# Hybrid encoder step on one core: two weights' splits moved ahead of the first evictions

## The chip, the core and the metric

The kernel is one launch on one core of a Trainium2 chip. The metric is the device time of that launch in microseconds (us). Most executions of one kernel agree within about 0.3%. The engines are TensorE (PE: matmuls; PEld: its weight loads), VectorE (DVE), ScalarE (ACT), GpSimd (POOL) and SyncE (SP). Each works through its own queue in order. SP and POOL issue the DMAs of this kernel's weights.

## What is computed

One step of an encoder layer, for a prompt of 512 rows and a sample of 64 rows, 576 rows side by side:

```python
x += mixer(rmsnorm(x))        # gated DeltaNet branch || GLA branch, gated merge
x += cross_attn(rmsnorm(x))   # 4 heads into 256 memory tokens
x += conv_ffn(rmsnorm(x))     # up-projection, causal conv, gate, down-projection
y  = rmsnorm(x)
```

This study deals with the first 45 us. There `h = rmsnorm(x)` (model width 1024) and `proj = h @ w_in` begin, whose columns are q, k, v, z and so on, by heads of 128. The first three products are q, k and v of head 0, the fourth is z of head 0, and the fifth and sixth are value heads of the GLA branch. A narrow product of 32 columns (gates and low-rank gate input) stands between the third and the fourth.

## The kernel before

**Tiles.** Activations lie transposed: 8 tiles of 128 features x 576 rows. Every operand of a projection is kept as a high and a low part (`h` rounded to fp32r, `lo` the rest), and a product is made of three: high x high, high x low of the activation, low x high of the weight. A weight of 128 columns is 8 blocks of 128x128, so one tile of 128x1024 for `h` and one for `lo`. The 576 columns go as 256 and 320 into two PSUM banks, so a projection is 8 blocks x 3 x 2 = 48 matmuls. The norm's factor per row is applied when a product is evicted, so products of the first norm don't wait for it.

**How a weight is made** (`emit_weight`, `split_summed`). SP loads it into a raw tile (`wr`, 4 buffers). ACT writes `-raw`, rounded, into `lo` (ACTIVATE in the trace) and then `raw`, rounded, into `h` (CAST). POOL then issues a DMA from HBM that adds the weight onto `lo` (`w<-wt` in the trace), so that what is left in `lo` is the weight less `h`. The weight tiles (`w`) have 6 buffers, so three weights at a time. A new weight's tile has to wait until TensorE has read what lay in that buffer. The first three weights are split by ACT and DVE alone, in six halves beside the loads of x.

```python
def split_summed(h, lo, raw, src):
    A.activation(lo, raw, AF.Copy, scale=-1.0)
    A.copy(h, raw)
    drv.accumulate(lo, src, nc.gpsimd)
```

**Order.** Instructions are not issued where they are written. A driver (`Driver`) keeps a model of when each operand is ready and each engine free, puts each instruction into a heap with its modelled start, and empties the heap in that order (line 292, to which the profile puts nearly everything). So the code's order fixes what the model may see, and the model fixes the order on each engine. `pending` holds the tiles that are still in use for the driver: `drop` gives tiles back, `fetch` emits the next weights as long as fewer than 6 weight tiles are in use, and `weight` drops the tiles of weights that went before and emits what is missing.

**The start** (`main`, from line 1760). `first3` are the PSUM tiles of the first three products. They run with the block k as the outer loop, and the weights are repacked so that the first weight tile holds what the first 48 of the 144 matmuls need, the second the next 48, the third the last 48. Behind them `conv_raw` evicts the three products (two by DVE, one by ACT, tiles `u`), `fetch(3)` asks for more weights, and `sq_act` squares the last four tiles of x (ACT) and adds them up into `acc` (DVE). `c_rstat` makes the norm's factors: matmuls of `acc` with ones, `rin` (DVE), the power `rt` (POOL), two diagonal tiles `dg` (DVE), matmuls of `dg` with ones, and `rbc` (ACT). `c_first` then makes `ba` (DVE) from the narrow product and `rbc`, and `c_gates` multiplies it on TensorE (`sm<-cst,ba` and `sm<-ba,wg`).

At `fetch(3)` all 6 weight tiles are still in use for the driver, so it emits nothing. The fourth, fifth and sixth weight are emitted when the fourth product (`za`) asks for its weight, which is after the evictions, the squares and the narrow product in the code.

Of the kernel before, what the change touches and what calls it, by code (L numbers as in the profile page):

```python
# [22 lines left out]
KT = D // P  # L23
# [489 lines left out]
def tile_trunk(ctx, tc, xT, memT, wt, wd, vec, cst, w0, wgate, st_gdn, st_conv, st_gla, st_ffn, ckT, cv,  # L513
# [23 lines left out]
    def slot(s="s", dt=F32, w=SLOT):  # L537
        return drv.rotate("s", NS, sp.tile([P, w], dt, tag="s", name=nm(s)))
# [36 lines left out]
    def f(ap):  # L575
        return ap.bitcast(F32)
# [3 lines left out]
    wready = {}  # L580
# [5 lines left out]
    def drop(*aps):  # L586
        for ap in aps:
            drv.pending.discard((ap if hasattr(ap, "tensor") else ap[:]).tensor.name)

    def raw_tile():  # L590
        while all(n in drv.pending for tag in ("raw", "rawf") for n in drv.ring.get(tag, ())) and len(drv.ring.get("raw", ())) == RAWB:
            make(next(iter(unmade)))
        if fp is not None and drv.first("rawf", RF, "raw", RAWB):
            return keep(drv.rotate("rawf", RF, fp.tile([P, 1024], F32, tag="rawf", name=nm("wr"), bufs=RF)))
        return keep(drv.rotate("raw", RAWB, wp.tile([P, 1024], F32, tag="raw", name=nm("wr"), bufs=RAWB)))
# [3 lines left out]
    def w_tile():  # L599
        if fp is not None and drv.first("wf", WF, "w", WB):  # L600
            t_ = drv.rotate("wf", WF, fp.tile([P, 1024], F32R, tag="wf", name=nm("w"), bufs=WF))
        else:
            t_ = drv.rotate("w", WB, wp.tile([P, 1024], F32R, tag="w", name=nm("w"), bufs=WB))
        wnames.add(t_[:].tensor.name)
        return keep(t_)
# [8 lines left out]
    def defer(i, fn, at):  # L614
        if i < LATE0:
            fn()
            return
        unmade[i] = fn
        drv.later(at, lambda: make(i))

    def emit_weight(i, at=0.0):
        kind, idx = WORDER[i]
        if kind == "*":
            wready[i] = emit_product(i, at, *idx)
            return
        raw = raw_tile()
        n = 1024
        if kind == "dn":
            m, p = idx
            n = len(PARTS[p]) * 128  # L630
            src = wd[m, :, PART0[p] * 128:PART0[p] * 128 + n]
        elif kind in ("outa", "outb"):
            n, c = 512, 512 * (kind == "outb")
            src = wt[WIDX[("out", idx)], :, c:c + 512]
        else:
            src = wt[WIDX[(kind, idx)]]
        DMA(raw[:, :n], src)
        h = w_tile()
        h, lo = (h[:, 0:512], h[:, 512:1024]) if n <= 512 else (h[:], w_tile()[:])
        summed = kind in SUMMED and (kind, idx) != ("dn", (7, 3))  # L640

        def split_():
            if summed:
                split_summed(h[:, :n], lo[:, :n], raw[:, :n], src)
            else:
                A.copy(h[:, :n], raw[:, :n])
                X.tensor_tensor(lo[:, :n], raw[:, :n], f(h[:, :n]), op=ALU.subtract)
            drop(raw[:])

        defer(i, split_, max(drv.ready_at(raw[:, :n]), at - (LEADD if summed else LEADV)))  # L650
        wready[i] = (h, lo)
# [5 lines that stand above are left out]
# [76 lines left out]
    def fetch(i, now=None):  # L733

        now = i if now is None else now
        room = WB + (WF if fp is not None else 0)
        for j in range(i, len(WORDER)):
            if j in wready:
                continue
            if j >= wlimit[0]:  # L740
                break
            kd_, i_ = WORDER[j]
            if len(drv.pending & wnames) + (1 if kd_ in ("*", "outa", "outb") or kd_ == "dn" and len(PARTS[i_[1]]) <= 4 else 2) > room:
                break
            emit_weight(j, drv.now + WPRE[j] - WPRE[now])
# [24 lines left out]
    for k in range(KT):  # L770
# [3 lines left out]
        if k in WPART:  # L774
            i, a, b = WPART[k]
# [25 lines left out]
    def mm3(outs, wh, wl, a, b, k, first, last):  # L801
        ch = wh[:, k * 128:(k + 1) * 128]
        cl = wl[:, k * 128:(k + 1) * 128]
        for o, c in outs:
            PE.matmul(o, ch, a[:, c], start=first, stop=False)
        for o, c in outs:
            PE.matmul(o, ch, b[:, c], start=False, stop=False)
        for o, c in outs:
            PE.matmul(o, cl, a[:, c], start=False, stop=last)
# [198 lines left out]
    def conv_parts(u, *ts):  # L1008
        return list(zip((u[:, 3:259], u[:, 259:515], u[:, 518:582]), *((t_[:, 0:256], t_[:, 256:TP], t_[:, TP:T]) for t_ in ts)))

    def bank_parts(ps):
        return ps[:, 0, 0:256], ps[:, 1, 0:256], ps[:, 1, 256:320]

    def conv_raw(ps, copy):
        u = slot("u")
        for (o,), i in zip(conv_parts(u), bank_parts(ps)):
            copy(o, i)
        return u
# [692 lines left out]
    def main():  # L1711
# [12 lines left out]
        def sq_act(k):  # L1724
            o = acc if k == 0 else slot("sq")
            A.activation(o[:, 0:T], x[k][:, 0:T], AF.Square)
            if k:
                V.tensor_tensor(acc[:, 0:T], acc[:, 0:T], o[:, 0:T], op=ALU.add)
# [33 lines left out]
        for k in range(KT):  # L1762
            for i, ps in enumerate(first3):
                n, b = divmod(3 * k + i, 8)
                mm3([(ps[:, 0, 0:256], slice(0, 256)), (ps[:, 1, 0:320], slice(256, T))], *ws[n], *xs[k], b, k == 0, k == KT - 1)
        raw_u = [conv_raw(ps, copy) for ps, copy in zip(first3, (V.tensor_copy, V.tensor_copy, A.copy))]
        fetch(3)
        for k in range(4, KT):
            sq_act(k)
        drv.spawn(c_rstat("n1", [(acc, 0)], 4, True, 0.0))  # L1770
        pa, pb_ = sm(), sm()
        for o, c in ((pa[:, 0:256], slice(0, 256)), (pb_[:, 0:320], slice(256, T))):
# [702 lines left out]
    def c_mem_stat():  # L2475
# [12 lines left out]
        drv.spawn(c_rstat("nm", [(macc, 0)], 2, False, 11.0, mbc_t))  # L2488

    drv.run(main())  # L2490


# [114 lines left out]
```

## Time and profile before

| | us |
|---|---|
| median of 3 runs | 1081.94 |
| lowest and highest run | 1079.63, 1083.07 |
| time of the profiled execution | 1078.61 |
| its span in the trace | 1076.8 |
| PE busy | 1065.5 (99% of the span) |
| DVE busy | 751.3 (70%) |
| ACT busy | 706.9 (66%) |
| POOL busy | 363.4 (34%) |
| mean granted TensorE clock | 0.997 |

The span runs from the first to the last instruction of the trace. Busy shares say little by themselves here, since the stages differ. The views used below are these: the list of waits (who waited for whom, with total, count and longest), the timeline (start, duration, engine, instruction, and in square brackets the idle time before it and what ended it), the windows (busy time in a stretch of the span, the granted clock, and the load of the DMA engines), and the chain of work that ended last, followed back from the end. `sm` are PSUM banks, `xh` and `xl` the high and low part of an activation, `w` a weight tile, `wr` a raw weight, `wt` the weights in HBM. Rows such as `x2` or `x12` merge instructions that follow each other.

### The profile page before, as it was taken

Reading aid. Unit: us, or ns where it says so; the run is one execution under the profiler, and the core shown is the slowest. Engines: PE = TensorE matmul, PEld = TensorE weight load, DVE = VectorE, ACT = ScalarE, POOL = GpSimd, SP = SyncE. Lnnn points to the kernel's source line nnn. Section 1 sums busy time; section 2 is a strip of 40 time slices with the busy share of each in tenths; the row PEclk is TensorE's granted clock in tenths of the full one; section 3 lists DMA queues with packets and bytes.
Section 4 is the critical chain, followed back from the end, with each engine's and each line's share of the span. In section 5 each row is a group of like instructions: output and inputs, shape, how many; then the busy total and the mean of one; then the engine's idle time right before and its main releaser. Section 6 shows DMA issues by size and latency. Waiting matters only on the chain.

```text
span 1076.8 us, 21403 instructions
## 1 busy us (share of the span) xinstructions
PE 1065.5 (99%) x8162; PEld 1048.5 (97%) x8162; DVE 751.3 (70%) x1472; ACT 706.9 (66%) x1410; POOL 363.4 (34%) x584
## 2 busy tenths in 40 slices
PE   9899999999999999999999999999999999999997
PEld 8899999999999999999999999999999999999997
DVE  6666854767665776878647766778877776678665
ACT  6665546564667577456666678768776775777645
POOL 0334225344434333114211235344343333332324
PEclk9999999999999999999999999999999999999999
DMA  7656354454437979679674368758887798778844
GB/s 270 158 124 154 61 135 110 95 123 106 99 58 167 252 171 199 237 208 238 172 186 138 63 161 198 180 115 166 185 192 173 153 217 189 181 159 190 185 87 109
DMA packets 68182, 171.33 MB, mean 159 GB/s; under 512 B 7920, under 2 KB 14576, under 8 KB 68080
## 3 DMA queue, kind: packets, MB, share of 16 engines
q0 software_dynamic: 30672, 71.19, 38.4%
q1 hardware_dynamic: 36976, 98.26, 27.6%
q8 instruction: 64, 1.05, 0.4%
q10 hardware_dynamic: 432, 0.53, 0.1%
q14 instruction: 38, 0.31, 0.1%
HBM read 157.50 MB, written 5.37 MB: 151 GB/s over the span
## 4 chain that ended last, share of the span: by engine, by line
PE 95%; DMA 2%; ACT 1%; DVE 1%; issue 0%; POOL 0%; ACTq 0%; DVEq 0%; POOLq 0%
PE sm L292 95%; DMA w<-wt 2%; ACT w L292 1%; PE warm L292 0%; DVE on L292 0%; ACT jk L292 0%; DVE ws L292 0%; DVE x L292 0%; DVE gt L292 0%; DVE acl L292 0%; DVE yo L292 0%; ACT ao L292 0%; DVE S L292 0%; ACT ach L292 0%; ACT xh L292 0%
## 5 line engine op out<-in xcount | busy, mean ns | idle before, releaser
L292 PE MATMUL sm<-xh,w 128*128 128x290 f32 (+3 forms) x2304 | 448.6, 301 | 3.7 <-DMA w<-wt 3.2
L292 PEld LDWEIGHTS sm<-xh,w 128*128 128x128 f32 x2304 | 358.8, 190 | 6.2 <-DMA w<-wt 3.7
L292 PE MATMUL sm<-xl,w 128*128 128x290 f32 (+3 forms) x1152 | 270.6, 296 | 0.0
L292 POOL DMA_DIRECT2D w<-wt x152 | 135.1, 898 | 348.3 <-ACT w L292 296.5
L292 PE MATMUL sm<-ach,w 128*128 128x288 f32 (+2 forms) x1212 | 231.4, 296 | 0.2 <-DVE x L292 0.2
L292 PEld LDWEIGHTS sm<-xl,w 128*128 128x128 f32 x1152 | 200.7, 189 | 0.2 <-DVE xl L292 0.2
L292 PEld LDWEIGHTS sm<-ach,w 128*128 128x128 f32 x1212 | 189.8, 188 | 1.2 <-ACT w L292 0.6
L292 ACT CAST w<-wr 128x512 fp32r<-128x512 f32 (+5 forms) x209 | 159.2, 764 | 15.2 <-PE sm L292 9.6
L292 ACT ACTIVATE w<-wr 128x512 fp32r<-128x512 f32 (+5 forms) x186 | 142.2, 765 | 27.0 <-PE sm L292 25.8
L292 PE MATMUL sm<-acl,w 128*128 128x256 f32 (+2 forms) x606 | 146.6, 295 | 0.2 <-DVE acl L292 0.2
L292 ACT CAST w<-ws 128x512 fp32r<-128x512 f32 (+1 forms) x136 | 80.2, 597 | 49.9 <-DVE ws L292 26.9
L292 PEld LDWEIGHTS sm<-acl,w 128*128 128x128 f32 x606 | 107.3, 188 | 0.5 <-DVE acl L292 0.5
L292 DVE TENSOR_TENSOR w<-ws,w 128x512 fp32r<-128x512 f32 (+1 forms) x107 | 72.8, 689 | 22.6 <-ACT w L292 20.8
L292 DVE SCALAR_TENSOR_TENSOR fc<-fu,vec,fc 128x578 f32<-128x578 f32 x88 | 70.5, 816 | 3.3 <-ACT fc L292 3.3
L292 PE MATMUL sm<-sh,w 128*128 128x290 f32 x288 | 61.5, 298 | 0.0
L292 DVE TENSOR_TENSOR x<-x,sm 128x320 f32<-128x320 f32 (+3 forms) x98 | 40.1, 438 | 22.8 <-PE sm L292 22.5
L292 POOL DMA_DIRECT2D w<-wd x34 | 29.8, 886 | 75.1 <-ACT w L292 67.6
L292 ACT ACTIVATE fc<-fu,vec 128x578 f32<-128x578 f32 x44 | 38.1, 871 | 15.1 <-POOL fu L292 14.8
L292 PEld LDWEIGHTS sm<-sh,w 128*128 128x128 f32 x288 | 47.6, 189 | 0.0
L292 PE MATMUL sm<-oh,w 128*128 128x256 f32 (+1 forms) x256 | 44.8, 295 | 0.0
L292 DVE TENSOR_TENSOR ws<-ws,wr 128x512 f32<-128x512 f32 (+1 forms) x66 | 43.8, 663 | 1.0
L292 PE MATMUL sm<-sl,w 128*128 128x290 f32 x144 | 39.7, 297 | 0.0
(391 smaller groups left out, 1947.9 us busy)
## 6 DMA issues: line engine op xcount, KB each, us to landing
wr<-wt SPq DMA_DIRECT2D x129, 512.0 KB, 5.6
w<-wt POOLq DMA_DIRECT2D x51, 512.0 KB, 6.7
w<-wt POOLq DMA_DIRECT2D x101, 256.0 KB, 6.1
w<-ws POOLq DMA_DIRECT2D x27, 256.0 KB, 5.1
x<-xT SPq DMA_DIRECT2D x16, 288.0 KB, 5.9
wr<-wt SPq DMA_DIRECT2D x14, 256.0 KB, 5.2
wr<-wd SPq DMA_DIRECT2D x8, 448.0 KB, 5.0
w<-wd POOLq DMA_DIRECT2D x8, 448.0 KB, 6.7
```

The source lines that it names most:

```text
L292: fn(*args, **kw)
```

## The change

Directly behind the first three products, and ahead of their evictions, the code now squares the last four tiles of x, gives the six tiles of the first three weights back, and emits the fourth and fifth weight (`emit_weight(3)`, `emit_weight(4)`: load, ACTIVATE, CAST, adding DMA). `fetch(3)`, behind the evictions, now finds room for two tiles and emits the sixth weight.

```diff
                 mm3([(ps[:, 0, 0:256], slice(0, 256)), (ps[:, 1, 0:320], slice(256, T))], *ws[n], *xs[k], b, k == 0, k == KT - 1)
+        for k in range(4, KT):
+            sq_act(k)
+        for i in range(3):
+            drop(*wready.pop(i))
+        emit_weight(3)
+        emit_weight(4)
         raw_u = [conv_raw(ps, copy) for ps, copy in zip(first3, (V.tensor_copy, V.tensor_copy, A.copy))]
         fetch(3)
-        for k in range(4, KT):
-            sq_act(k)
         drv.spawn(c_rstat("n1", [(acc, 0)], 4, True, 0.0))
```

No instruction is added or removed. The order on PE and on SP is the same as before; on ACT, DVE and POOL it differs only within the first part of the program.

On ACT, behind the last squares, the rows were these. `u_313` is the eviction of the third product, `w_357` and `w_356` are `lo` and `h` of the fourth weight, `w_360` and `w_359` of the fifth, `w_363` and `w_362` of the sixth, and `rbc` is the norm's factor:

```order
L292 ACTIVATE sq_317<-x_89 128x576
L292 COPY u_313<-sm_135 128x256
L292 COPY u_313<-sm_136 128x256
L292 COPY u_313<-sm_136 128x64
L292 ACTIVATE w_357<-wr_355 128x1024
L292 CAST w_356<-wr_355 128x1024
L292 ACTIVATE w_360<-wr_358 128x1024
L292 CAST w_359<-wr_358 128x1024
L292 ACTIVATE w_363<-wr_361 128x1024
L292 CAST w_362<-wr_361 128x1024
L292 COPY rbc_430<-sm_431 128x512
```

Now the same place on ACT reads as follows (`w_317` and `w_316` are the fourth weight, `w_320` and `w_319` the fifth, `w_326` and `w_325` the sixth, `u_323` the eviction):

```order
L292 ACTIVATE sq_314<-x_89 128x576
L292 ACTIVATE w_317<-wr_315 128x1024
L292 CAST w_316<-wr_315 128x1024
L292 ACTIVATE w_320<-wr_318 128x1024
L292 CAST w_319<-wr_318 128x1024
L292 COPY u_323<-sm_135 128x256
L292 COPY u_323<-sm_136 128x256
L292 COPY u_323<-sm_136 128x64
L292 ACTIVATE w_326<-wr_324 128x1024
L292 CAST w_325<-wr_324 128x1024
L292 COPY rbc_428<-sm_429 128x512
```

The splits of the fourth and fifth weight stand ahead of the eviction of the third product instead of behind it. Their writes into the weight tiles wait for TensorE's 48th and 96th matmul of the first three products, the last readers of the buffers.

On POOL, behind the first memsets, the rows were these (`DMA w_...` are the adding DMAs of the three weights, `rt` is the norm's power, `ISA` a set-up instruction ahead of it, `scm` a mask for the gates):

```order
L292 MEMSET rin_353 128x8
L292 DMA w_357<-wt 128x1024
L292 ISA
L292 TENSOR_TENSOR rt_341<-rin_353,mhalf 128x5
L292 DMA w_360<-wt 128x1024
L292 DMA w_363<-wt 128x1024
L292 MEMSET u_311 128x3
L292 COPY u_311<-cstin 128x3
L292 MEMSET u_312 128x3
L292 COPY u_312<-cstin 128x3
L292 MEMSET bt 128x40
L292 MEMSET scm_479 128x576
```

Now POOL has there:

```order
L292 DMA w_317<-wt 128x1024
L292 MEMSET rin_366 128x8
L292 DMA w_320<-wt 128x1024
L292 MEMSET u_321 128x3
L292 DMA w_326<-wt 128x1024
L292 ISA
L292 TENSOR_TENSOR rt_353<-rin_366,mhalf 128x5
L292 COPY u_321<-cstin 128x3
L292 MEMSET u_322 128x3
L292 COPY u_322<-cstin 128x3
L292 MEMSET bt 128x40
L292 MEMSET scm_467 128x576
```

All three DMAs now stand ahead of `rt`, two of them stood behind it, and the small copies and memsets follow `rt` directly. On DVE the last addition into `acc` stands ahead of the six copies `u<-sm` instead of behind them.

## The prediction

> **What bounds the kernel now.** I read the page first, then TensorE's waits, then the timeline at the place of the change. The page says who sets the end:
>
> ```profile
> PE 1065.5 (99%) x8162; PEld 1048.5 (97%) x8162; DVE 751.3 (70%) x1472; ACT 706.9 (66%) x1410; POOL 363.4 (34%) x584
> ```
>
> TensorE is busy for 1065.5 us, 99% of the span, so only two things can be won: stretches in which it stands, and stretches in which it runs slowly. The list of TensorE's waits names what it stood for (total, count, longest):
>
> ```profile
> PE sm L292 <- DMA w<-wt: 3.2, 2, 2.8
> ```
>
> One wait of 2.8 us holds nearly all of it, for a weight's adding DMA. TensorE's timeline shows where, and what came next:
>
> ```profile
> 32.63 0.43 PE L292 MATMUL sm<-xl,w 128*128 128x256 f32 x2
> 35.90 0.80 PE L292 MATMUL sm<-xh,w 128*128 128x256 f32 x4 [2.84 <-DMA w<-wt]
> 36.54 0.77 PE L292 MATMUL sm<-dg,onesr 128*128 128x512 f32 x4
> 37.15 3.18 PE L292 MATMUL sm<-xh,w 128*128 128x256 f32 x12
> 40.12 1.41 PE L292 MATMUL sm<-cst,ba 128*128 128x8 f32 x10
> 41.46 2.38 PE L292 MATMUL sm<-ba,wg 128*128 128x512 f32 x8
> 43.64 0.51 PE L292 MATMUL sm<-xh,w 128*128 128x256 f32 x2
> ...
> 47.96 2.54 PE L292 MATMUL sm<-xh,w 128*128 128x256 f32 x18
> 50.34 0.43 PE L292 MATMUL sm<-xl,w 128*128 128x256 f32 x2
> ```
>
> The fourth product's `h` part ends at 33.06, and its `lo` part starts at 35.90, so TensorE stands for 2.84 us. The second cost is hidden in busy time. The 12 matmuls at 37.15 take until 40.12, which is 248 ns each. The 18 of the same kind at 47.96 take until 50.34 (the start of the next row), 132 ns each. The windows of 1 us (busy time, granted clock, share and GB/s of the DMA engines) say why:
>
> ```profile
> 37.00:38.00 1.00, 1.00 (x7) 0.60 1.08 254
> 38.00:39.00 1.00, 1.00 (x6) 0.50 1.02 291
> 39.00:40.00 1.00, 1.00 (x6) 0.50 1.02 270
> 40.00:41.00 1.00, 1.00 (x9) 0.69 1.09 279
> ```
>
> The clock was granted at half from about 37.2 to 40.6: with 0.60 the first us holds 0.8 us at half, and with 0.69 the last holds 0.62, so 3.4 us in all. I take this as the echo of the stall. The chain of work shows what the stall hung on:
>
> ```profile
> 26.19 0.96 ACT w L292
> 27.16 0.31 issue
> 27.46 8.39 DMA w<-wt
> ```
>
> Here ACT, behind the eviction of the third product, writes `-raw` of the fourth weight, POOL issues the adding DMA at 27.46, and that lands 8.39 us later.
>
> **What the change removes and moves.** It adds and removes no instruction. On ACT it moves four of these operations:
>
> ```profile
> 15.62 4.12 ACT L292 ACTIVATE sq<-x 128x576 f32<-128x576 f32 x7
> 25.43 0.77 ACT L292 COPY u<-sm 128x256 f32<-128x256 f32 x3 [5.69 <-PE sm L292]
> 26.07 1.08 ACT L292 ACTIVATE w<-wr 128x1024 fp32r<-128x1024 f32 x1
> 27.03 1.05 ACT L292 CAST w<-wr 128x1024 fp32r<-128x1024 f32 x1
> ```
>
> ACT ends its squares at 19.74 and then stands for 5.69 us. Two weights of about 1.95 us each (the ACTIVATE at 26.07 to the CAST's end at 28.08 is 2.01) fit there: they would end near 23.7 and leave 1.7 us before the eviction at 25.43. So the eviction isn't delayed, and that idle time is the cover. Without it, each weight in front would delay the eviction by 2 us. Two things must be there by then. The buffers are free: the writes wait for the 48th and 96th of the 144 matmuls of the first three products, which end just ahead of the eviction at 25.43, so at about a third and two thirds of their way. And the raw weights must have landed; the loads that SP issued (start, and time to landing):
>
> ```profile
> L292 SPq DMA_DIRECT2D wr<-wt x1: 328/328/328, 13.5 to 13.5; - x1
> DMA to landing us min/median/max: 5.0/5.0/5.0
> L292 SPq DMA_DIRECT2D wr<-wt x2: 328/352/376, 14.3 to 14.7; - x2
> DMA to landing us min/median/max: 6.5/6.9/7.3
> ```
>
> The fourth weight lands at 18.5, the fifth at 14.3 + 6.5 = 20.8, the sixth at 14.7 + 7.3 = 22.0. ACT would want them at 19.7, 21.7 and 26.1, so none is late.
>
> The adding DMA of the fourth weight thus leaves POOL at about 19.74 + 1.08 + 0.3 (the issue of the chain) = 21.1, and that of the fifth near 23. With the 8.39 us of the chain the first lands at 29.5; the slowest of the next two needed 12.0 us:
>
> ```profile
> L292 POOL DMA_DIRECT2D w<-wt x2: 913/929/945, 30.4 to 31.2; - x2
> DMA to landing us min/median/max: 9.4/10.7/12.0
> ```
>
> Even then it lands at 33.1, when TensorE comes to it at 33.06. **The 2.84 us go.** The fifth weight's `lo` is wanted only behind 16 pairs of `h` matmuls (47.96 before), the sixth's still later. SP's loads into the freed raw tiles follow the CASTs, so they too go out earlier, and they share the engines with two adding DMAs instead of three.
>
> **The half clock goes with it.** At 132 ns the 12 matmuls take 1.59 instead of 2.97 us, which is 1.38 less. The 10 small ones at 40.12 still run half a us at half clock, which is worth at most 0.25. I take 1.45 together. By the clock's own end it would be 3.4 x 0.5 = 1.7, the upper end; the lower is 0, if the echo stays or is absent in most executions.
>
> Of the clock, the Trainium skill ("TensorE: Matmul & The Clock Gate", section "Part 1: The HAM clock gate (the "warmup" mystery)") says that TensorE falls to half speed after at least one idle window of about 3.4 us. The row differs: a stall of 2.84 us was enough, or the half clock has another cause. By the page at its word this echo would not be the stall's, and the sum would hold the stall alone; I follow the trace, since this is the only half-speed stretch behind the only long stall.
>
> **What is late next.** Once the stall is gone, TensorE meets `dg` and `ba` earlier. The rows of POOL, DVE and ACT:
>
> ```profile
> 27.46 1.05 POOL L292 DMA_DIRECT2D w<-wt  x1 [24.57 <-ACT w L292]
> 29.20 1.19 POOL L292 TENSOR_TENSOR rt<-rin,mhalf 128x5 f32<-128x5 f32 x1 [0.69 <-DVE rin L292]
> ...
> 31.77 0.52 POOL L292 MEMSET u<- 128x3 f32 x1
> ...
> 33.29 0.19 POOL L292 COPY u<-cstin 128x3 f32<-128x3 f32 x1
> ```
>
> ```profile
> 31.32 0.25 DVE L292 TENSOR_SCALAR dg<-keep,rh 128x64 fp32r<-128x64 f32 x1
> ...
> 32.08 1.12 DVE L292 TENSOR_SCALAR dg<-keep,rl 128x64 fp32r<-128x64 f32 x1
> ```
>
> ```profile
> 37.20 0.70 ACT L292 COPY rbc<-sm 128x512 f32<-128x512 f32 x2 [5.34 <-PE sm L292]
> 37.82 0.82 DVE L292 TENSOR_TENSOR ba<-sm,rbc 128x256 f32<-128x256 f32 x2 [4.62 <-ACT rbc L292]
> ```
>
> `rt` now stands behind the sixth weight's DMA on POOL. That DMA can go at 27.46 as the fourth's did before (same place on ACT, behind the eviction), so POOL is free at 28.51, and `rt` waits for `rin` until 29.20 as it does now: slack 0.69. Without that, `dg` and everything behind it would be late by what is missing.
>
> `dg` is complete at 32.08 + 1.12 = 33.20. TensorE would want it at 33.06 + 4 x 0.132 = 33.59: slack 0.39. But POOL's small work, 31.77 to 33.48, now follows `rt` at once and lies beside all four `dg` operations, not the last alone. Two equal TENSOR_SCALARs took 0.25 and, beside POOL's memsets, 1.12. If all 1.71 us of POOL's work held DVE up, `dg` would end at 32.08 + 0.25 + 1.71 = 34.04, 0.45 too late; if none did, at 32.33. Lower end 0, upper end 0.45. I take 0.1, near the 0.87 that one such meeting cost. Then TensorE has 0.61 us of `dg` matmuls and 1.59 of `lo` matmuls, 2.20 in all, while `ba` needs 38.64 - 36.54 = 2.10 us from the start of the `dg` matmuls. This slack of 0.1 is the thinnest; a late `ba` would cost what is missing, us for us.
>
> The Trainium skill's "GPSIMD Engine Reference", section "8. Key points", says that GpSimd shares its SBUF interfaces with VectorE and contends with DVE instructions that have two SBUF inputs or run in a two-port mode. It speaks against the change at this place. The pair 0.25 and 1.12 agrees; by it the sum would lose up to the 0.45 above.
>
> On DVE the last `acc` addition moves from behind the copies of `u` to ahead of them, into time in which DVE stood waiting for the products: nothing. Behind 43.64 each step waits for TensorE or for work that TensorE released, so it moves along.
>
> **Sum:** 2.85 (33.06 to 35.90, rounded) + 1.45 - 0.10 = 4.2 us. The profiled execution took 1078.61 us, so 1074.4 on its terms. It lies 3.3 us below the median of the three runs, 1081.94, and I forecast the median: **1077.7 us**, 0.39% less.
>
> **Rivals.**
>
> A new wait at `dg` or `ba`: POOL's work holds DVE up fully, and `rt` is 0.4 late on top. For it: slacks of 0.39 and 0.1 only. Against it: most of POOL's items are of 3 columns. Gain 4.2 - 0.8 = 3.4, so 1078.5.
>
> The half clock isn't the stall's, or shows in few executions. For it: the stall lies across the boundary of whatever is counted, and the clock fell 1.3 us after work had resumed. Gain 2.85 - 0.1 = 2.75, so 1079.2. The Trainium skill's rule above would lead here.
>
> It doesn't do what it says: the transfer lands at 35.9 anyway, having started 6.4 us earlier. It would need 14.8 us; the slowest row is 12.0. Time 1081.9.
>
> Slower: POOL's queue. `rt` now waits behind an adding DMA that waits for ACT, and ACT for the raw load of the fifth weight. Up to a delay of 0.69 + 0.39 = 1.08 us nothing is lost; beyond that TensorE stands before `dg`, and from 1.08 + 4.2 = 5.3 us on the kernel is slower. A delay of 8.5 us, with its own half clock, would give about 1081.9 - 4.2 + 7.4 = 1085. Against it: the load has to land 1.7 + 0.9 + 5.3, some 8 us later than 20.8.
>
> **How the numbers follow.** The forecast has 0.66, the new wait 0.12, the stall alone 0.15, no effect 0.03, slower 0.04. About 0.3% (3.2 us) is what a measurement of this kernel can tell from no change. The forecast lies 1 us beyond it and the runs before spread by 3.4 us, so I count 0.85 of the forecast, half of the new wait and a quarter of the stall alone as faster: 0.56 + 0.06 + 0.04 = 0.66. Slower has 0.04, which leaves 0.30. The range: the largest gain, 2.85 + 1.7 = 4.6, from the lowest run gives 1075.0; the smallest, 2.85 - 0.45 = 2.4, from the median plus 1.5 of scatter gives 1081.0.
>
> **What would show it.** In the changed profile, ACT's ACTIVATE of the fourth weight starts near 19.8 and POOL's first adding DMA near 21.1, landing by 30. TensorE has no idle time near 33, the granted clock stays at 1.00 to 45, and the matmuls at 43.64 come near 39.4. `dg` ends near 33.2. The forecast is wrong if TensorE stands before `dg` or `cst,ba` for over 1 us, if a stretch at half clock remains, or if a later wait of TensorE appears that takes the time back.

## The result

| us | before | changed |
|---|---|---|
| median of 6 runs | 1080.79 | 1073.84 |
| lowest and highest | 1078.95, 1083.63 | 1073.46, 1074.27 |
| profiled execution | 1078.61 | 1073.90 |
| its span | 1076.8 | 1072.1 |

The ratio is 0.9934 (95% interval 0.9916 to 0.9951), 6.95 us less by the medians. The two profiled executions differ by 4.71 us only. The forecast of 4.2 us was made on the profiled one and then taken from the median, and the measured median lies 1.2 us below the lower end of the range (1075.0). So two things have to be explained: what the 4.7 us of the profiles are, and where the other 2.2 us of the medians come from. The scatter shrank too, from 4.7 to 0.8 us.

TensorE's list of waits in the changed kernel (total, count, longest) no longer has the long one:

```profile
PE warm L292 <- POOL acc L292: 1.0, 1, 1.0
PE sm L292 <- ACT gt L292: 0.4, 1, 0.4
PE sm L292 <- DMA w<-wt: 0.4, 1, 0.4
```

The first is the program's start. TensorE's timeline at the place of the former stall:

```profile
32.63 0.43 PE L292 MATMUL sm<-xl,w 128*128 128x256 f32 x2
32.89 0.69 PE L292 MATMUL sm<-xh,w 128*128 128x256 f32 x4
33.42 0.77 PE L292 MATMUL sm<-dg,onesr 128*128 128x512 f32 x4
34.03 1.83 PE L292 MATMUL sm<-xh,w 128*128 128x256 f32 x12
35.69 1.16 PE L292 MATMUL sm<-cst,ba 128*128 128x8 f32 x10
36.79 2.38 PE L292 MATMUL sm<-ba,wg 128*128 128x512 f32 x8
38.97 0.51 PE L292 MATMUL sm<-xh,w 128*128 128x256 f32 x2
```

No row has an idle time behind it. The `lo` part starts at 32.89 instead of 35.90, 3.01 us earlier. From there to the gates' small matmuls it takes 2.80 instead of 4.22 us (1.42 less), and from those to the fifth weight's matmuls 3.28 instead of 3.52 (0.24 less). Together that is 4.67 us, the whole difference of the spans (4.7). Behind 39 us the work only moved along. The granted clock (behind the count of matmuls) stays whole:

```profile
36.00:37.00 1.00, 1.00 (x9) 1.00 0.02 8
37.00:38.00 1.00, 1.00 (x5) 1.00 0.00 0
38.00:39.00 1.00, 1.00 (x6) 1.00 0.00 0
```

The causes stand in ACT's, POOL's and DVE's timelines:

```profile
15.30 4.12 ACT L292 ACTIVATE sq<-x 128x576 f32<-128x576 f32 x7
19.32 1.05 ACT L292 ACTIVATE w<-wr 128x1024 fp32r<-128x1024 f32 x1
...
25.42 0.77 ACT L292 COPY u<-sm 128x256 f32<-128x256 f32 x3 [2.23 <-PE sm L292]
```

```profile
20.68 1.05 POOL L292 DMA_DIRECT2D w<-wt  x1 [17.83 <-ACT w L292]
...
29.20 1.20 POOL L292 TENSOR_TENSOR rt<-rin,mhalf 128x5 f32<-128x5 f32 x1 [0.90 <-DVE rin L292]
...
30.72 0.57 POOL L292 MEMSET scm<- 128x576 f32 x1
31.24 0.09 POOL L292 MEMSET u<- 128x3 f32 x1
```

```profile
30.73 0.68 DVE L292 TENSOR_TENSOR dg<-keep,rh 128x512 fp32r<-128x512 f32 x1
...
32.10 0.25 DVE L292 TENSOR_SCALAR dg<-keep,rl 128x64 fp32r<-128x64 f32 x1
34.70 0.82 DVE L292 TENSOR_TENSOR ba<-sm,rbc 128x256 f32<-128x256 f32 x2 [2.36 <-ACT rbc L292]
```

The split starts at 19.32, its adding DMA leaves POOL at 20.68 instead of 27.46, and the eviction still starts at 25.42, behind 2.23 us of idle time. The norm's power `rt` starts at 29.20 as before. `dg` ends at 32.35, earlier than before (33.20).

### The profile page after: what moved, and what is told of

It reads as the page before. It is cut to its first block, busy times and chain, and to the rows that moved or that the text cites. A ratio compares the mean times of both kernels' runs of the same rounds, so it can differ in the third digit from the quotient of the medians.

```text
span 1072.1 us, 21402 instructions
## 1 busy us (share of the span) xinstructions
PE 1063.7 (99%) x8162; PEld 1047.1 (98%) x8162; DVE 750.1 (70%) x1472; ACT 706.7 (66%) x1410; POOL 363.7 (34%) x584
## 4 chain that ended last, share of the span: by engine, by line
PE 96%; ACT 1%; DMA 1%; DVE 1%; issue 0%; POOL 0%; ACTq 0%; DVEq 0%; POOLq 0%
PE sm L292 96%; DMA w<-wt 1%; ACT w L292 1%; PE warm L292 0%; DVE on L292 0%; ACT jk L292 0%; DVE ws L292 0%; DVE x L292 0%; DVE gt L292 0%; DVE acl L292 0%; DVE yo L292 0%; ACT ao L292 0%; DVE S L292 0%; ACT ach L292 0%; ACT xh L292 0%
```

## The experiments

The question was why executions of the kernel before differ by up to 5 us and those of the changed one do not. Three theories: the half clock lasts for more stretches in some executions (A), the transfer and so the stall is longer in some (B), or the time is lost elsewhere (C). Besides that, each part of the change was run alone.

**The kernel before again**, no edit.

> The kernel before, unchanged, to see what makes its executions differ: they ran from 1078.95 to 1083.63 us, while those of the changed kernel stayed within 0.8 us. Theory A (the half clock): after the stall TensorE stays at half clock for one, two or three stretches of 3.4 us, each worth up to 1.7 us, so slower executions have a lower mean granted clock (one stretch more is 0.0016 of 1077 us) at about the same stall of 2.8 us. Theory B (the transfer): the adding DMA takes longer in some executions, so the stall in the trace is longer than 2.84 us and the clock is the same. Theory C (elsewhere): the stall and the clock near 33 to 41 us are as in the first profile in a slow execution too, and the extra time is found behind 45 us.

Its 12 executions had a median of 1078.74 us (1078.08 to 1082.07; ratio 0.9993, interval 0.998 to 1.0006). Each execution comes with its mean granted clock. With the other executions of this kernel on the three chips of the experiments, 76 in all, times and clocks go together:

| mean granted clock | executions | median us | lowest, highest |
|---|---|---|---|
| 0.999 | 3 | 1077.02 | 1076.85, 1077.08 |
| 0.998 and 0.997 | 48 | 1078.5 | 1077.98, 1079.33 |
| 0.996 | 14 | 1079.51 | 1078.74, 1080.11 |
| 0.995 | 5 | 1081.99 | 1081.55, 1082.07 |
| 0.993 | 6 | 1083.41 | 1083.08, 1083.85 |

This is what theory A says, and B and C don't: from 0.999 to 0.993 is 0.006 x 1080 = 6.5 us of clock, and the times differ by 6.4 us. The agreement is rougher than it looks. The means are rounded to 0.001, and in every profile they also hold a fall to half clock behind TensorE's last matmul, where it costs nothing: in the kernel before from 1074.86 us to the end of the span at 1076.8, in the changed one from 1068.40 to 1072.1, which takes 0.0009 and 0.0017 off the mean. That is why 0.998 can stand for an execution with one stretch behind the stall and for one with none. This run's own profile has a stall of 3.31 us and one stretch, from 36.66 to 40.07.

**TensorE kept at work through the stall.** The edit adds matmuls between the fourth product's two parts, into a bank whose content has been read (the main part of it; two more places set `NFILL` to 12 and keep the bank as `spare`):

```diff
+            if NFILL and N.get("spare") is not None:
+                bank = N.pop("spare")
+                for _ in range(NFILL):
+                    drv.put(drv.now, [(nc.tensor.matmul, (bank, ones_r, ones_r.unsqueeze(1).broadcast_to([P, 4, 128])), dict(start=True, stop=True))])
             for k in range(n):
```

> The kernel before with 12 more matmuls of 128x512 on TensorE, between the fourth product's h part and its lo part, into a bank that nobody reads any more: about 12 x 0.216 = 2.6 us, so TensorE works through the stall but still waits for the transfer. If the half clock is the stall's echo, it is gone: 1.4 to 1.7 us less than before in the profile (span near 1075.3), the matmuls behind the stall at 132 ns. Theory A adds that the scatter of the kernel before goes too: all executions within 1 us, near 1077. Theory B: the scatter stays, 1077 to 1082. If the half clock has another cause, nothing changes.

The median was 1077.37 us (12 runs, 1076.43 to 1078.02; ratio 0.9981, interval 0.997 to 0.9991). TensorE's timeline:

```profile
32.52 2.90 PE L293 MATMUL sm<-onesr 128*128 128x512 f32 x12
35.90 0.79 PE L293 MATMUL sm<-xh,w 128*128 128x256 f32 x4 [0.48 <-DMA w<-wt]
36.53 0.77 PE L293 MATMUL sm<-dg,onesr 128*128 128x512 f32 x4
37.14 1.83 PE L293 MATMUL sm<-xh,w 128*128 128x256 f32 x12
38.80 1.17 PE L293 MATMUL sm<-cst,ba 128*128 128x8 f32 x10
```

The transfer lands as late as before (35.90), but the 12 matmuls behind it take 1.66 us (37.14 to 38.80) instead of 2.97. All 12 executions had a clock of 0.998 or more, and they lie within 1.6 us, where the kernel before on this chip spread from 1077.02 to 1083.85. So the half clock, and most of the scatter, are the stall's: busy work in its place removes them and leaves the wait for the transfer, 3.4 us by this median and that of the next run. The time is 0.35 us above the median of the three executions of the kernel before at 0.999.

**Only the fourth weight ahead** (edit against the changed kernel).

```diff
         emit_weight(3)
-        emit_weight(4)
```

> The change with the fourth weight alone given ahead (the line for the fifth weight left out). If the stall hangs on the fourth weight's transfer only, this is as fast as the changed kernel: 1073.8, within 0.5 us, no idle time of TensorE near 33 us. If the fifth weight's earlier split is worth something by itself, it is slower by 0.5 us or more, with a wait of TensorE for an adding DMA near 43 us.

Median 1073.97 us (6 runs, 1073.28 to 1074.14; ratio 0.9948, interval 0.9929 to 0.9966). That is the changed kernel's time, and TensorE waited for no adding DMA near 43 us. The fifth weight's early split adds nothing that can be measured.

**Only the squares ahead.**

```diff
+        for k in range(4, KT):
+            sq_act(k)
         raw_u = [conv_raw(ps, copy) for ps, copy in zip(first3, (V.tensor_copy, V.tensor_copy, A.copy))]
         fetch(3)
-        for k in range(4, KT):
-            sq_act(k)
```

> The change with the last squares ahead alone, no weight given ahead. The orders on ACT, PE, POOL and SP are those of the kernel before; on DVE one addition into acc stands ahead of the copies. My steps cost this at nothing: the same time as before, with the same scatter, a stall near 2.84 us. If the moved squares carry part of the gain, it is 0.5 us or more below before.

Median 1078.68 us (12 runs, 1078.06 to 1080.41; ratio 0.9998, interval 0.9986 to 1.0009): nothing, as expected.

**Three more profiled executions of the kernel before**, no edit.

> The kernel before, unchanged, one more profiled execution, to catch one of those whose mean clock is 0.996 or less (16 of 53 timed executions of this kernel and of the one with the squares alone were, at 1078.9 to 1083.9 us). Theory A1: the half clock follows the stall directly and lasts two to four stretches of 3.4 us, over the small matmuls for the gates at 40 to 44 us and beyond; the stall itself is as long as in the other profiles (2.8 to 3.5 us). Theory A2: the further stretches lie elsewhere in the program, far from the stall. Theory B: the stall is longer by the extra time. At a clock of 0.997 or more: one stretch, as in the profiles so far.

> As the run before it: the kernel before, one more profiled execution. Theory A1: half clock in one go behind the stall, two to four stretches of 3.4 us in a slow execution. Theory A2: further stretches elsewhere. Theory B: a longer stall.

> As the two runs before it: the kernel before, one more profiled execution. Theory A1: half clock in one go behind the stall, two to four stretches of 3.4 us in a slow execution. Theory A2: further stretches elsewhere. Theory B: a longer stall.

They took 1076.85, 1083.36 and 1077.08 us, at clocks of 0.999, 0.993 and 0.999, both ends of the table. TensorE in the first:

```profile
35.85 0.81 PE L292 MATMUL sm<-xh,w 128*128 128x256 f32 x4 [2.80 <-DMA w<-wt]
36.50 0.77 PE L292 MATMUL sm<-dg,onesr 128*128 128x512 f32 x4
37.10 1.84 PE L292 MATMUL sm<-xh,w 128*128 128x256 f32 x12
38.78 1.17 PE L292 MATMUL sm<-cst,ba 128*128 128x8 f32 x10
39.87 2.38 PE L292 MATMUL sm<-ba,wg 128*128 128x512 f32 x8
42.06 0.52 PE L292 MATMUL sm<-xh,w 128*128 128x256 f32 x2
```

and in the second, with its windows of 1 us below:

```profile
36.10 1.33 PE L292 MATMUL sm<-xh,w 128*128 128x256 f32 x4 [3.29 <-DMA w<-wt]
37.23 1.32 PE L292 MATMUL sm<-dg,onesr 128*128 128x512 f32 x4
38.36 3.23 PE L292 MATMUL sm<-xh,w 128*128 128x256 f32 x12
41.38 2.02 PE L292 MATMUL sm<-cst,ba 128*128 128x8 f32 x10
43.34 4.53 PE L292 MATMUL sm<-ba,wg 128*128 128x512 f32 x8
47.63 0.83 PE L292 MATMUL sm<-xh,w 128*128 128x256 f32 x2
```

```profile
35.00:36.00 1.00, 0.00 (x0) 0.80 1.05 279
36.00:37.00 1.00, 0.90 (x4) 0.50 1.05 274
...
48.00:49.00 1.00, 1.00 (x6) 0.50 0.85 147
49.00:50.00 1.00, 1.00 (x8) 0.88 1.01 201
```

The transfer lands 0.25 us later, at 36.10 instead of 35.85. All the rest is the clock: half from about 35.6 to 49.24, which is 0.4 + 13 + 0.24 = 13.6 us, four times 3.41. The fifth weight's matmuls come at 47.63 instead of 42.06, 5.57 us later, of the 6.5 us between the two executions' times; the others at half clock until 49.24 make up 0.7 more. Theory A1 holds: one go, directly behind the stall. The third execution has a stall of 2.80 us and no half clock, as the first.

**Half the filler** (edit against the run with 12).

```diff
-NFILL = 12
+NFILL = 6
```

> The kernel before with 6 filler matmuls in the stall instead of 12: TensorE works 1.3 us of it and stands for 1.4 to 2 us. If every idle time of this size brings the clock down, the times are those of the kernel before (median 1078.8, clock 0.997, some executions at 0.996 or less). If it takes most of a 3.4 us stretch without work, the half clock is gone in nearly all executions: median 1077.4, clock 0.998 to 1.0, as with 12 fillers. In between, a part of the executions would show it, by where the idle time lies in the stretches.

Median 1076.75 us (11 runs, 1076.4 to 1079.05; ratio 0.9983, interval 0.9974 to 0.9992). The profiled execution stood for 1.97 us with no half clock:

```profile
36.22 0.80 PE L293 MATMUL sm<-xh,w 128*128 128x256 f32 x4 [1.97 <-DMA w<-wt]
```

Nine executions lie at 1077.13 us or below, two at 1078.58 and 1079.05. So by the times about 2 us of idle time bring the clock down in some executions, about 3 us in nearly all. What decides is worked out in the last section.

**The changed kernel again**, beside the kernel before on one chip.

> The changed kernel, unchanged, beside the kernel before on one chip. By the profiles the stall and the later start of the fourth product's lo part are worth 3.0 us in every execution, and the half clock 0, 1.7, 3.4 ... up to 6.6 us by how many stretches an execution has. So: 1073.9 within 0.5 us, no execution slower than 1075, clock 0.998 to 1.0 throughout; against a kernel before that lies at 1077 (no half clock), 1078.6 (one stretch) and up to 1083.9 (four).

Median 1073.51 us (6 runs, 1072.95 to 1073.9), all at a clock of 0.999 or 1.0. The 17 executions of the kernel before had a median of 1078.55 (1078.23 to 1083.19). The ratio is 0.9948 (0.9934 to 0.9962), 5.0 us: the whole gain of a chip on which most executions have one stretch.

**Only the weights ahead**, the squares where they were.

```diff
+        for i in range(3):
+            drop(*wready.pop(i))
+        emit_weight(3)
+        emit_weight(4)
         raw_u = [conv_raw(ps, copy) for ps, copy in zip(first3, (V.tensor_copy, V.tensor_copy, A.copy))]
```

> The change with the two weights given ahead, but the last squares left where they were in the code, behind the evictions. The driver then puts two of the four squares behind three weights' splits on ACT, and TensorE's matmuls of acc with ones and of dg behind the fourth product's h part and lo part. If the squares were only moved along, the time is that of the changed kernel. My reading: the norm's chain becomes late, from acc's matmuls to dg it takes 5.7 us (27.54 to 33.20 before), so TensorE stands about 2.5 us before dg and 1.5 us before the gates' small matmuls: 1078 or more, with the half clock in a part of the executions.

Median 1077.95 us (12 runs, 1076.78 to 1079.22; ratio 0.9991, interval 0.998 to 1.0001): nearly all of the gain is lost. ACT, then TensorE, then its windows of 1 us:

```profile
27.58 1.27 ACT L292 ACTIVATE sq<-x 128x576 f32<-128x576 f32 x2
```

```profile
31.50 1.08 PE L292 MATMUL sm<-keep,acc 128*128 128x1 f32 x10
32.44 2.37 PE L292 MATMUL sm<-xh,w 128*128 128x256 f32 x16
35.83 0.47 PE L292 MATMUL sm<-dg,onesr 128*128 128x512 f32 x1 [1.02 <-DVE dg L292]
36.50 0.64 PE L292 MATMUL sm<-dg,onesr 128*128 128x512 f32 x3 [0.20 <-DVE dg L292]
38.18 2.16 PE L292 MATMUL sm<-cst,ba 128*128 128x8 f32 x10 [1.04 <-issue]
40.27 4.53 PE L292 MATMUL sm<-ba,wg 128*128 128x512 f32 x8
```

```profile
38.00:39.00 1.00, 0.82 (x4) 0.50 0.00 0
...
44.00:45.00 1.00, 1.00 (x5) 0.59 0.95 188
```

The driver puts two squares behind three weights' splits, so `acc` is complete late, its matmuls stand behind the `h` part, and TensorE waits 1.02 us for `dg` (I had expected 2.5) and 1.04 (expected 1.5) before the gates' matmuls, which want `ba` from the same chain. The small matmuls at 40.27 take 4.53 us instead of 2.38, at half clock. The stall for the transfer is traded for one for the norm.

## Why the prediction was right or wrong

**The stall: right.** It was put at 2.85 us and gave 3.01 (the 0.16 more is that matmuls in a row overlap by 0.17 us, 33.06 against 32.89, which the idle time doesn't hold), for the reason given: ACT had 5.69 us of idle time, the raw weight was there, and the DMA left POOL 6.8 us earlier (forecast 21.1, measured 20.68).

**The half clock: right in its cause, wrong in its size.** It was a term of 1.45 us with an upper end of 1.7, which is one stretch of 3.4 us. In the profiled execution it was 1.42 + 0.24 = 1.66. Over the executions it is none to four stretches: 1077.0 us without any, 1083.4 with the longest, 6.4 us apart. The executions at 0.996 and 0.995 weren't profiled, so how many stretches those have is not shown. The 12 fillers show that it hangs on the stall. The prediction called it the only half-speed stretch; the trace has a second one behind TensorE's last matmul, from 1074.86, which costs nothing.

**From the profile to the median: the step that failed.** On the profiled execution's terms the forecast was 1074.4, and 1073.9 was measured. Then the 4.2 us were taken from 1081.94, a median of three runs that lay 3.3 us above the profiled time, as if that difference would stay. Of the 3.86 us between the forecast of 1077.7 and the measured 1073.84, 3.33 are this difference and about 0.5 the sum's. In the sum's own terms the half clock was sized by one execution with one stretch, and by their times the executions behind the median had lost more to it. Two of those three runs, 1081.94 and 1083.07, have the times of the table's rows at 0.995 and 0.993, and 1083.63 of the next three as well; their clocks weren't recorded, so this is read from the times. The extra belonged to the stall, and went with it. The range's lower end, the largest gain of 4.6 from the lowest run, missed that the gain is larger in the executions that take longer; from that lowest run, 1079.63, it was 5.8 us.

**The cover on ACT: right.** The eviction wasn't delayed. That both weights had to go ahead was not claimed, and one is enough.

**The squares: only half seen.** The prediction cost the one addition that moved on DVE at nothing, which is right by itself. It didn't see what the move is needed for: without it the driver orders two of the squares behind the splits, and nearly all of the gain is gone. The forecast was right here without the reason.

**What is late next: a little too dear.** A wait of 0.1 us was put at `dg` and `ba`, up to 0.45, and none came. POOL's small work took from 30.37 to 31.33, 0.96 us instead of 1.71, and the last TENSOR_SCALAR of `dg` came behind it, at 0.25 us. `ba` is complete at 34.70 + 0.82 = 35.52, 0.17 us before TensorE wants it; the forecast had 0.1 there.

**The rivals.** The new wait, the missing effect and POOL's queue didn't show; `rt` starts at 29.20 in both kernels. The stall without its half clock exists, but as 3 of 76 executions of the kernel before, and the gain against those is 3.2 us. What the prediction said for that rival, a stall across the boundary of whatever is counted, is what the traces of two of those three show.

## What to carry to other kernels

When runs of one kernel scatter, ask whether the profiled execution is a quick or a long one, and put the mean granted clock of each execution beside its time, before an effect worked out on one execution is taken from a median. A stall of TensorE can cost more than its length, here 3 us and then up to 13.6 us at half clock, differently from execution to execution, so a stall of that size in dense work can be worth more than its idle time, and dummy matmuls in its place tell the two apart. When code is handed ahead to a driver that orders by a model, everything that its new place could displace has to be handed ahead as well.

## What was not expected of the hardware

The half clock came in whole stretches of 3.41 us: none, one, two (with only the weights ahead) or four. The stall's length doesn't decide: it was 2.80 us in both profiled executions with no half clock, and 2.84 to 3.49 in those with one stretch. The traces show what does. In five profiles the clock falls near the stall and again behind TensorE's last matmul. The two falls are 1037.65 us apart in four of them and 1044.48 in the execution with four stretches, and these distances differ by 6.83 us, two stretches. They are 304 and 306 times 3.413 us. So the clock changes only at the boundaries of a grid with that step, which isn't set by the stall. Where there is no fall near the stall, the boundary is an estimate, 1037.65 us back from the fall at the end:

| profiled execution | TensorE idle (us) | boundary | idle in the step up to it, in the next | half clock |
|---|---|---|---|---|
| before | 33.06 to 35.90 | 37.21 | 2.1, 0 | one stretch |
| before again | 32.73 to 36.03 | 36.66 | 2.8, 0 | one |
| only the squares | 32.75 to 36.23 | 36.84 | 2.8, 0 | one |
| before, second of three | 32.81 to 36.10 | 35.59 | 2.8, 0.5 | four |
| only the weights | three waits | 37.98 | 2.1, 0.2 | two |
| before, first of three | 33.05 to 35.85 | 34.18 | 1.1, 1.7 | none |
| before, third of three | 33.20 to 36.00 | 34.52 | 1.3, 1.5 | none |
| half the filler | 34.25 to 36.22 | 36.03 | 1.8, 0.2 | none |

The clock fell where 2.1 us or more of a step were idle, and not where 1.8 or less were; the two stalls of 2.80 us without half clock are cut in two by a boundary. The end of the changed kernel fits: its last matmul ends at 1066.13, and the clock falls at 1068.40, with 2.3 us idle. No run moved a stall along the grid on purpose, so the limit between 1.8 and 2.1 us rests on these profiles alone.

The Trainium skill ("TensorE: Matmul & The Clock Gate", section "Part 1: The HAM clock gate (the "warmup" mystery)") says that the activity window is free-running and about 3.4 us long, which agrees with the grid. It also asks for a whole idle window of that length; here 2.1 us of it were enough, and with only the weights ahead two waits of about 1 us and one of 0.2.

How long the half clock lasts is open. The clock stayed at half behind four steps, and each of them held 0.2 to 0.5 us of idle time or about 1 us or more of the gates' 128x8 matmuls; a step filled by `ba,wg` alone ended in whole clock (41.40 to 44.81 with only the weights ahead). Whether the 128x8 matmuls keep the clock down was not tried.

Beside POOL's memset of 576 columns DVE's TENSOR_TENSOR with two inputs took its usual 0.68 us, while before the TENSOR_SCALAR beside the same memset, and beside POOL's small copies, took 1.12 instead of 0.25.
